# Attention block with two branches: inverse row sums of the last head pair spread by GpSimd and transposed into PSUM, in place of a way through DRAM

## Chip, cores and metric

One NeuronCore of one Trainium2 chip. The metric is device time in microseconds of one execution; the kernel before has three runs.

## What is computed

A block over 512 positions of width 1024. The input is RMS-normalised and projected once; eight heads of forgetting attention (fox) and eight heads of block-sparse attention (moba) follow, each with a SiLU gate, and the two results are projected, gated and added:

```python
proj = rms_norm(x, norm_g) @ w_in
y_fox  = from_heads(fox_attention(q, k, v, log_f)) * jax.nn.silu(fz)
y_moba = from_heads(moba_attention(q, k, v)) * jax.nn.silu(mz)
merged = (sigmoid(ga + b_gate[0]) * (y_fox @ w_fox)
          + sigmoid(gb + b_gate[1]) * (y_moba @ w_moba))
x = x + merged @ w_out
```

With 512 positions and blocks of 256, each moba query sees its own block up to itself and all blocks before it, so both branches are causal softmax attention here. Heads are 64 wide.

## The kernel before

**Precision.** Every matmul operand is split into a high part (rounded by a ScalarE copy, `wh`, `pth`, `yh`) and a low part (a VectorE subtraction, `wl`, `ptl`, `yl`), and a product is three matmuls, high by high, high by low, low by high (two where one operand is stacked).

**Order of the work.** Work is written as a list of units that are interleaved by hand: four attention groups of four heads (fox a, fox b, moba a, moba b), each mixed with projection units as filler, then the gates (`GA`, `GB`), the moba projection (`wm`, matmul tile `pm`) and the output (`wo`, tile `po`). The framework's scheduler then fixes each engine's own queue, which the engine runs strictly in order. The last group's end is interleaved with the first gate product.

**An attention group** handles two pairs of heads, `pr` 0 and 1. For each head, `Aa` makes logits and exponentials `p` with their row sums `rsum`; after each pair, VectorE takes the reciprocals `rinv`, as a column per head and query tile (queries on partitions). `Bb` transposes the exponentials on TensorE in three groups (`p_a` four blocks, `p_b` four, `p_cc` two), splits each (L582, L583), and multiplies them with the values into the bank `pv` (L586, L587). Its two halves are added (`ysh` L611, L612) into `ypair`: 128 partitions are two heads by 64 dimensions, columns are the 512 queries. `Yp` multiplies `ypair` by the SiLU gate `ZS` and the inverse sums, and splits the result into `yh` (L628) and `yl` (L629).

**The inverse sums have to be turned.** `rinv` has queries on partitions; `ypair` has them on columns. So `sums_out` transposes eight columns of `rinv` on TensorE (`p_ri`, L555), copies them out (L557) and stores them to a DRAM tile (L558, 4 KB); `sums_in` loads them back twice with a broadcast over 64 partitions (L566, 128 KB each, ScalarE's queue) into `rinv_bc`. For most pairs GpSimd multiplies gate and sums (L626); for the last pair of the last group VectorE does.

**The gates** use products of half-matrices with sums of them (Strassen-Winograd form: seven products for eight). A product `n` runs 24 matmuls of 128x256 (L715, L717, L718) on one of three PSUM banks, `pb1` to `pb3`. The left sides are the normalised input (`Gh`, `Gl`) and four sums `S0` to `S3`, which GpSimd's queue loads from DRAM (L258) as the attention's tiles become free. ScalarE copies a bank out before it is used again (`e_GA`, L725), VectorE adds it to another (L728). Weights come by SP's queue (L684) into four buffers, are combined by VectorE (L679) and split by L110 on ScalarE and L112 on VectorE, into four further buffers which the products free.

Of the kernel before, what the change touches and what calls it, by code (L numbers as in the profile page):

```python
# [7 lines left out]
F32 = mybir.dt.float32  # L8
F32R = mybir.dt.float32r
AF = mybir.ActivationFunctionType  # L10
OP = mybir.AluOpType
AX = mybir.AxisListType

P = 128
S = 512
D = 1024
NT = S // P
KT = D // P
HD = 64
# [10 lines left out]
def fox_moba_kernel(ctx: ExitStack, tc, xT, x, w_in, w_fl, w_fox, w_moba, w_out, cst, rope, out):  # L30
# [3 lines left out]
    V, A, G, T = nc.vector, nc.scalar, nc.gpsimd, nc.tensor  # L34
# [6 lines left out]
    stage = {}  # L41
# [7 lines left out]
    def t2(tag, bufs, name, shape=(P, 512), dt=F32):  # L49
        pool = stage["pool"] if tag in ("qs", "pt", "pc", "ys") else sb  # L50
        return pool.tile(list(shape), dt, name=name, tag=tag, bufs=bufs)

    def pst(tag, bufs, name):
        return ps.tile([P, 512], F32, name=name, tag=tag, bufs=bufs)
# [4 lines left out]
    def tp(name):  # L59
        return pst("tp", 3, name)  # L60
# [10 lines left out]
    ident = con.tile([P, P], F32, name="ident")  # L71
# [121 lines left out]
    r = con.tile([P, NT], F32, name="r")  # L193
# [191 lines left out]
    ZS = {}  # L385
# [94 lines left out]
    ri = con.tile([P, 16, 4], F32, name="rinv")  # L480
    R_dram = dr.tile([16, NT, P], F32, name="r_dram")

    def attn_group(br, half, gq, gk):
        fox = br == "f"
        qn, kn = QN[f"{br}q{half}"], QN[f"{br}k{half}"]
        hb = 4 * (half == "b") + (0 if fox else 8)
        last = br + half == "mb"
        st = {}
# [32 lines left out]
        def Aa(h):  # L521
            def go():
                qs, kh, kl, q2 = st[h]
                hh = hb + h
                pts = []
                for i in range(NT):
                    n = P * (i + 1)
                    lg = pst("lg", 2, "lg")
                    qt = slice(i * P, (i + 1) * P)
                    T.matmul(lg[:, :n], qs[:, qt], kh[:, :n], start=True, stop=False)  # L530
                    T.matmul(lg[:, :n], q2[:, qt], kl[:, :n], start=False, stop=True)  # L531
                    pt = stage["pool"].tile([P, n], F32, name=f"p{i}", tag=f"p{i}", bufs=2)
                    V.tensor_tensor_reduce(pt, lg[:, :n], mask[:, 512 - n:512], -0.125, 3.0e38,  # L533
                                           op0=OP.add, op1=OP.min, accum_out=mkn[:, hh, i:i + 1])
                    A.activation(pt, pt, AF.Exp, bias=mkn[:, hh, i:i + 1], scale=-1.0,  # L535
                                 accum_out=rs[:, hh, i:i + 1])
                    pts.append(pt)
                st[h] = pts
                if h % 2:
                    inverse_sums(h // 2)  # L540
                elif h:
                    sums_in(0)
            return go
# [8 lines left out]
        def sums_out(pr):  # L552
            h0 = hb + 2 * pr
            p = tp("p_ri")
            T.transpose(p[:8, :P], ri[:, h0:h0 + 2, :].rearrange("p h t -> p (h t)"), ident)  # L555
            rt = sb.tile([8, P], F32, name="rinv_t", tag="rinv_t", bufs=1)
            A.activation(rt, p[:8, :P], AF.Copy)  # L557
            A.dma_start(out=R_dram[h0:h0 + 2].rearrange("h t p -> (h t) p"), in_=rt)  # L558

        def sums_in(pr):  # L560
            if last and pr:
                rb = st["r", pr] = t2("u", 4, "rinv_bc")
            else:
                rb = st["r", pr] = stage["pool"].tile([P, S], F32, name="rinv_bc", tag="rinv_bc", bufs=1)
            for o in range(2):
                A.dma_start(out=rb[o * HD:(o + 1) * HD, :],  # L566
                            in_=R_dram[hb + 2 * pr + o].rearrange("t p -> (t p)").partition_broadcast(HD))

        def Bb(h):
            def go():  # L570
                pts, vt = st[h], VT[f"{br}v{half}"]
                o = h % 2
                pv = pst("pv", 1, "pv")

                def blk(dst, i, j):
                    T.transpose(dst, pts[i][:, j * P:(j + 1) * P], ident)

                def spl(p, n):
                    tag, w, bufs = ("pt", 512, 4) if n == 512 else ("pc", 256, 2)
                    hi = t2(tag, bufs, "pth", (P, w), F32R)  # L580
                    lo = t2(tag, bufs, "ptl", (P, w), F32R)
                    A.activation(hi[:, :n], p[:, :n], AF.Copy)  # L582
                    V.tensor_tensor(out=lo[:, :n], in0=p[:, :n], in1=hi[:, :n].bitcast(F32), op=OP.subtract)  # L583
                    return hi, lo
                def pvm(j, hl, c0, n, start, stop):
                    T.matmul(pv[:, P * j:P * j + n], vt[:, j, h, :], hl[0][:, c0:c0 + n], start=start, stop=False)  # L586
                    T.matmul(pv[:, P * j:P * j + n], vt[:, j, h, :], hl[1][:, c0:c0 + n], start=False, stop=stop)  # L587
                pa = tp("p_a")
                for i in range(4):
                    blk(pa[:, i * P:(i + 1) * P], i, 0)  # L590
                pb = tp("p_b")
                for i in range(1, 4):
                    blk(pb[:, (i - 1) * P:i * P], i, 1)
                blk(pb[:, 384:512], 3, 3)
                ha = spl(pa, 512)
                hbb = spl(pb, 512)
                pc = tp("p_cc")
                for i in range(2, 4):
                    blk(pc[:, (i - 2) * P:(i - 1) * P], i, 2)
                hc = spl(pc, 256)  # L600
                pvm(0, ha, 0, 512, True, False)
                pvm(1, hbb, 0, 384, False, False)
                pvm(3, hbb, 384, 128, False, False)
                pvm(2, hc, 0, 256, False, True)
                pr = h // 2
                if o == 0:
                    st["y", pr] = t2("u", 4, "ypair") if last and pr else t2("ys", 1, "ypair")
                y = st["y", pr]
                me, ot = (slice(0, HD), slice(HD, P)) if o == 0 else (slice(HD, P), slice(0, HD))
                sh = t2("u", 4, "ysh")  # L610
                A.activation(sh[me, :], pv[ot, :], AF.Copy)  # L611
                V.tensor_tensor(out=y[me, :], in0=pv[me, :], in1=sh[me, :], op=OP.add)  # L612
                if o == 0:
                    sums_out(pr)
                elif pr:
                    sums_in(1)
            return go

        def Yp(pr):
            def go():  # L620
                y = st["y", pr]
                gp = 2 * (half == "b") + pr
                yh = t2("y", 15, f"yh{br}{gp}", dt=F32R)
                yl = t2("y", 15, f"yl{br}{gp}", dt=F32R)
                zr = st["r", pr]
                (V if (br, gp) == ("m", 3) else G).tensor_tensor(out=zr, in0=ZS[br, gp], in1=zr, op=OP.mult)  # L626
                V.tensor_tensor(out=y, in0=y, in1=zr, op=OP.mult)
                A.activation(yh, y, AF.Copy)  # L628
                V.tensor_tensor(out=yl, in0=y, in1=yh.bitcast(F32), op=OP.subtract)  # L629
                Y[br, gp] = (yh, yl)  # L630
            return go
# [376 lines left out]
```

## Time and profile before

| | |
|---|---|
| runs | 444.06, 443.63, 441.45 us; median 443.63 |
| profiled execution | 444.28 us, its span 442.5 us |
| mean granted TensorE clock | 0.996 |
| TensorE busy | 428.4 us (97%) |
| VectorE, ScalarE, GpSimd busy | 314.7, 262.5, 87.6 us |
| data moved | 56.40 MB, mean 127 GB/s |

The span runs from the first to the last instruction in the trace; the execution's own time has 1.8 us around it. In the views, PE is TensorE's matmuls, PEld its weight loads, DVE VectorE, ACT ScalarE, POOL GpSimd; SPq and ACTq are instructions that issue transfers. A row of waits reads: engine, tile and line that waited, arrow, what ended the wait, then microseconds in total, times, longest. In the chain and the timeline the first number is the start, the second the duration. A row of groups ends in busy time, mean nanoseconds of one, and idle time ahead.

### The profile page before, as it was taken

Reading aid. Unit: us, or ns where it says so; the run is one execution under the profiler, and the core shown is the slowest. Engines: PE = TensorE matmul, PEld = TensorE weight load, DVE = VectorE, ACT = ScalarE, POOL = GpSimd, SP = SyncE. Lnnn points to the kernel's source line nnn. Section 1 sums busy time; section 2 is a strip of 40 time slices with the busy share of each in tenths; the row PEclk is TensorE's granted clock in tenths of the full one; section 3 lists DMA queues with packets and bytes.
Section 4 is the critical chain, followed back from the end, with each engine's and each line's share of the span. In section 5 each row is a group of like instructions: output and inputs, shape, how many; then the busy total and the mean of one; then the engine's idle time right before and its main releaser. Section 6 shows DMA issues by size and latency. Waiting matters only on the chain.

```text
span 442.5 us, 8082 instructions
## 1 busy us (share of the span) xinstructions
PE 428.4 (97%) x3100; PEld 403.9 (91%) x3100; DVE 314.7 (71%) x563; ACT 262.5 (59%) x491; POOL 87.6 (20%) x106
## 2 busy tenths in 40 slices
PE   6999999999999999999999999987999999999996
PEld 5998899999999998899998878877999989989996
DVE  5559994777998869676956689928978786584311
ACT  5676544876777769887765876717655545531100
POOL 1059200224142950134621002200000000000000
PEclk9999999999999999999999999998999999999999
DMA  8962164424377413303304212663134405624231
GB/s 261 388 246 69 54 205 137 111 74 136 110 233 209 103 55 120 119 13 122 106 14 132 95 24 90 232 203 96 60 133 126 160 1 183 197 96 152 88 96 48
DMA packets 25991, 56.40 MB, mean 127 GB/s; under 512 B 3296, under 2 KB 11936, under 8 KB 25952
## 3 DMA queue, kind: packets, MB, share of 16 engines
q1 hardware_dynamic: 14528, 39.95, 27.4%
q10 hardware_dynamic: 10272, 11.74, 9.0%
q0 software_dynamic: 1152, 4.19, 2.8%
q8 instruction: 24, 0.39, 0.4%
q14 instruction: 15, 0.12, 0.1%
HBM read 46.27 MB, written 6.32 MB: 119 GB/s over the span
## 4 chain that ended last, share of the span: by engine, by line
PE 85%; ACT 6%; DMA 4%; DVE 2%; issue 1%; ACTq 0%; SPq 0%; DVEq 0%
PE pb_GB L718 3%; PE pb_GB L717 3%; PE pb_GB L715 3%; PE po L815 3%; PE po L817 3%; PE po L816 3%; PE pb_GA L715 2%; PE pb_GA L717 2%; PE pb_GA L718 2%; PE pv L587 2%; PE pv L586 2%; PE lg L530 2%; PE lg L531 2%; PE pm L644 2%; PE pm L645 2%; PE pm L646 2%
## 5 line engine op out<-in xcount | busy, mean ns | idle before, releaser
L535 ACT ACTIVATE p<-p,negm 128x128 f32<-128x128 f32 (+1 forms) x64 | 35.7, 558 | 12.5 <-DVE negm L533 11.2
L310 POOL TENSOR_TENSOR ff<-ss,mh 128x8 f32<-128x8 f32 x16 | 27.1, 1699 | 79.6 <-DVE ss L308 77.3
L533 DVE CUSTOM_DVE_ANT_0 p<-lg,mask 128x128 f32<-128x128 f32 (+1 forms) x64 | 30.5, 485 | 5.8 <-PE lg L531 5.6
L815 PE MATMUL po<-wh_wo,mgh 128*128 128x256 f32 x96 | 27.1, 282 | 0.0
L817 PE MATMUL po<-wh_wo,mgl 128*128 128x256 f32 x96 | 27.0, 282 | 0.0
L816 PE MATMUL po<-wl_wo,mgh 128*128 128x256 f32 x96 | 26.9, 281 | 0.0
L825 DVE TENSOR_TENSOR ot<-po,xr 128x256 f32<-128x256 f32 x16 | 6.6, 424 | 24.7 <-PE po L817 23.6
L110 ACT ACTIVATE wh_wo<-wr_wo 128x1024 fp32r<-128x1024 f32 x8 | 8.5, 1061 | 21.6 <-PE po L817 8.0
L530 PE MATMUL lg<-KH,QS 128*128 128x128 f32 (+1 forms) x64 | 20.7, 332 | 0.4 <-DMA KH<-KH 0.4
L112 DVE TENSOR_TENSOR wl_GB<-wr_gb,wh_GB 128x1024 fp32r<-128x1024 f32 x14 | 16.8, 1223 | 4.2 <-ACT wh_GB L110 3.3
L110 ACT ACTIVATE wh_GB<-wr_gb 128x1024 fp32r<-128x1024 f32 x14 | 14.6, 1059 | 8.6 <-PE pm L645 2.5
L612 DVE TENSOR_TENSOR ypair<-pv,ysh 64x512 f32<-64x512 f32 x16 | 11.0, 688 | 10.8 <-ACT ysh L611 10.7
L816 PEld LDWEIGHTS po<-wl_wo,mgh 128*128 128x128 f32 x96 | 18.1, 189 | 0.0
L815 PEld LDWEIGHTS po<-wh_wo,mgh 128*128 128x128 f32 x96 | 18.1, 189 | 0.0
L817 PEld LDWEIGHTS po<-wh_wo,mgl 128*128 128x128 f32 x96 | 18.1, 188 | 0.0
L715 PE MATMUL pb_GA<-Gh,wh_GA 128*128 128x256 f32 x48 | 14.3, 298 | 3.3 <-ACT e_GA L725 3.3
L112 DVE TENSOR_TENSOR wl_GA<-wr_ga,wh_GA 128x1024 fp32r<-128x1024 f32 x14 | 16.6, 1219 | 1.2 <-ACT wh_GA L110 1.1
L110 ACT ACTIVATE wh_GA<-wr_ga 128x1024 fp32r<-128x1024 f32 x14 | 14.5, 1054 | 4.5 <-DVE wr_ga L679 2.7
L504 DVE SCALAR_TENSOR_TENSOR QS<-p_qT,cs,QS 64x512 fp32r<-64x512 f32 x16 | 12.0, 750 | 6.6 <-ACT QS L503 6.2
L611 ACT ACTIVATE ysh<-pv 64x512 f32<-64x512 f32 x16 | 9.5, 593 | 9.8 <-PE pv L587 8.0
L112 DVE TENSOR_TENSOR wl_wo<-wr_wo,wh_wo 128x1024 fp32r<-128x1024 f32 x8 | 9.8, 1222 | 7.4 <-ACT wh_wo L110 7.4
L583 DVE TENSOR_TENSOR ptl<-p_a,pth 128x512 fp32r<-128x512 f32 x16 | 11.0, 687 | 5.1 <-ACT pth L582 5.0
(448 smaller groups left out, 1798.8 us busy)
## 6 DMA issues: line engine op xcount, KB each, us to landing
wr_ga<-in_w_in_dram SPq DMA_DIRECT2D x8, 512.0 KB
wr_gb<-in_w_in_dram SPq DMA_DIRECT2D x8, 512.0 KB
wr_wo<-in_w_out_dram SPq DMA_DIRECT2D x8, 512.0 KB
xt<-in_xT_dram SPq DMA_DIRECT2D x8, 256.0 KB
x<-in_x_dram SPq DMA_DIRECT2D x8, 256.0 KB
s_dramh<-sum_sh ACTq DMA_DIRECT2D x8, 256.0 KB
s_draml<-sum_sl ACTq DMA_DIRECT2D x8, 256.0 KB
KH<-KH ACTq DMA_DIRECT2D x16, 128.0 KB
```

The costliest lines, as they stand in the source:

```text
L110: A.activation(hi[:, :, 0:n], src, AF.Copy)
L112: eng.tensor_tensor(out=lo[:, q, 0:n], in0=src[:, q], in1=hi[:, q, 0:n].bitcast(F32), op=OP.subtract)
L310: G.tensor_tensor(out=f2, in0=ss.rearrange("p t h -> p (t h)"), in1=mh, op=OP.pow)
L530: T.matmul(lg[:, :n], qs[:, qt], kh[:, :n], start=True, stop=False)
L533: V.tensor_tensor_reduce(pt, lg[:, :n], mask[:, 512 - n:512], -0.125, 3.0e38, op0=OP.add, op1=OP.min, accum_out=mkn[:, hh, i:i + 1])
L535: A.activation(pt, pt, AF.Exp, bias=mkn[:, hh, i:i + 1], scale=-1.0, accum_out=rs[:, hh, i:i + 1])
L715: T.matmul(o, hi[:, k, cc], lh, start=(n < 3 and c == 0 and k == 0), stop=False, skip_group_check=True)
L717: T.matmul(o, hi[:, k, cc], ll, start=False, stop=False, skip_group_check=True)
L718: T.matmul(o, lo[:, k, cc], lh, start=False, stop=(k == 3), skip_group_check=True)
L815: T.matmul(p[:, :CW], gh[:, st], hi[:, k, :CW], start=(kk == 0), stop=False)
L816: T.matmul(p[:, :CW], gh[:, st], lo[:, k, :CW], start=False, stop=False)
L817: T.matmul(p[:, :CW], gl[:, st], hi[:, k, :CW], start=False, stop=(kk == KT - 1))
```

## The change

For the last pair of the last group (`last and pr`) alone, the way through DRAM is left out: no `sums_out`, no `sums_in`. In `Yp`, GpSimd copies each head's `rinv` columns, broadcast over 64 columns, into `rinv_w` (two copies of 128x256), TensorE transposes its four 128x128 blocks into a PSUM bank `p_rinv` of the tag `lg`, which the attention's logits no longer need, and VectorE multiplies the gate in place by that bank. All other pairs stay as they were.

```diff
         def sums_in(pr):
             if last and pr:
-                rb = st["r", pr] = t2("u", 4, "rinv_bc")
-            else:
-                rb = st["r", pr] = stage["pool"].tile([P, S], F32, name="rinv_bc", tag="rinv_bc", bufs=1)
+                return
+            rb = st["r", pr] = stage["pool"].tile([P, S], F32, name="rinv_bc", tag="rinv_bc", bufs=1)
...
-                if o == 0:
+                if o == 0 and not (last and pr):
                     sums_out(pr)
...
-                zr = st["r", pr]
-                (V if (br, gp) == ("m", 3) else G).tensor_tensor(out=zr, in0=ZS[br, gp], in1=zr, op=OP.mult)
+                if last and pr:
+                    zr, rb = ZS[br, gp], pst("lg", 2, "p_rinv")
+                    h0 = hb + 2 * pr
+                    rw = t2("u", 4, "rinv_w")
+                    for o in range(2):
+                        G.tensor_copy(rw.rearrange("p (t o d) -> p t o d", o=2, d=HD)[:, :, o, :],
+                                      ri[:, h0 + o, :, None].to_broadcast([P, NT, HD]))
+                    for t in range(NT):
+                        T.transpose(rb[:, t * P:(t + 1) * P], rw[:, t * P:(t + 1) * P], ident)
+                    V.tensor_tensor(out=zr, in0=zr, in1=rb, op=OP.mult)
+                else:
+                    zr = st["r", pr]
+                    G.tensor_tensor(out=zr, in0=ZS[br, gp], in1=zr, op=OP.mult)
                 V.tensor_tensor(out=y, in0=y, in1=zr, op=OP.mult)
```

Lines in the changed kernel are one less after the first edit, and ten more after `Yp`.

## The prediction

> **What bounds the kernel now.** I read the page first, then the waits of the whole span, then the chain of work that ended last and the stretches around the one place it leaves TensorE.
>
> ```profile
> span 442.5 us, 8082 instructions
> PE 428.4 (97%) x3100; PEld 403.9 (91%) x3100; DVE 314.7 (71%) x563; ACT 262.5 (59%) x491; POOL 87.6 (20%) x106
> ```
>
> TensorE is busy for 97% of the span, so only two things can shorten the kernel: less TensorE work, or one of its few gaps closed. The waits, longest first (the first row is TensorE's largest wait of the whole span; none of its waits after it, from 303 us on, is listed at all):
>
> ```profile
> PE pb_GA L715 <- ACT e_GA L725: 3.3, 1, 3.3
> ...
> ACT yhm L628 <- DVE ypair L627: 7.2, 2, 7.0
> ...
> DVE rinv_bc L626 <- DMA rinv_bc<-r_dram: 6.0, 1, 6.0
> ```
>
> Three waits, one cause. The chain shows the order (start, duration, piece):
>
> ```profile
> 284.39 0.28 ACT rinv_t L557
> 284.68 0.27 ACTq L558
> 285.00 1.09 ACT pth L582 x2
> 286.09 0.95 ACT wh_GA L110
> 287.06 1.23 DVE wl_GA L112
> 288.29 0.34 DVE ptl L583
> 288.68 0.40 PE pv L587
> 289.16 0.45 ACTq L566
> 289.65 6.68 DMA rinv_bc<-r_dram
> 296.42 0.70 DVE rinv_bc L626
> 297.15 0.70 DVE ypair L627
> 297.99 0.42 issue
> 298.41 1.99 ACT wh_GA L110 x2
> 300.40 0.49 ACT e_GA L725
> 300.93 0.58 PE pb_GA L715
> ```
>
> The load of the last pair's inverse sums takes 6.68 us. VectorE stands in its queue at L626 for it, ScalarE behind VectorE at the cast L628, and behind that cast stand two weight splits (L110) and the copy L725 that frees the PSUM bank of TensorE's next product. Nobody needs the attention result itself in a hurry: its first reader is a matmul at 345 us.
>
> ```profile
> L644 PE MATMUL pm<-yhm,wh_wm x32: 388/394/403, 345.1 to 394.4; 128*128 128x512 f32 x32
> ```
>
> The stall therefore harms only by what is queued behind it. It has an after-effect in the granted clock (the last columns of a stretch are clock, DMA share, GB/s):
>
> ```profile
> 297.60:300.90 3.30, 0.00 (x0) 0.00 (x0) 2.57 (x4) 3.02 (x5) 0.00 (x0) 0.94 0.00 0
> 300.90:304.00 3.10, 3.07 (x14) 3.07 (x15) 3.07 (x4) 2.70 (x3) 0.00 (x0) 0.51 0.52 153
> 304.00:305.45 1.45, 1.45 (x14) 1.45 (x13) 0.61 (x1) 0.00 (x0) 0.00 (x0) 1.00 0.81 243
> ```
>
> After 3.3 us with no matmul the clock is 0.51 for 3.1 us: 14 matmuls there, where the next 1.45 us holds 14 as well.
>
> **The change, part by part.** In the built program all engines keep their order except around this place. I go by the starts of TensorE's instructions in before:
>
> ```profile
> 282.29 0.40 PE L586 MATMUL pv<-pth,v_mvb 128*128 128x512 f32 x1
> ...
> 283.56 0.28 PE L718 MATMUL pb_GA<-Gh,wl_GA 128*128 128x256 f32 x1
> ...
> 283.92 0.47 PEld L576 LDWEIGHTS p_a<-ident,p 128*128 128x128 f32 x4
> ...
> 285.85 0.48 PE L586 MATMUL pv<-pth,v_mvb 128*128 128x512 f32 x1
> ...
> 288.90 0.28 PE L715 MATMUL pb_GA<-S0h,wh_GA 128*128 128x256 f32 x1
> ...
> 294.58 0.29 PE L715 MATMUL pb_GA<-S1h,wh_GA 128*128 128x256 f32 x1
> ...
> 305.45 0.28 PE L715 MATMUL pb_GA<-S2h,wh_GA 128*128 128x256 f32 x1
> ```
>
> From 288.90 to 294.58 stand 48 gate matmuls (1 + 24 + 23): 0.118 us each, undisturbed.
>
> *Removed ahead of the last head's products.* One transpose, the copy L557 and its store, 0.55 us of ScalarE's chain and about 0.1 of TensorE. The order with it changes: ScalarE now splits the three transposed blocks one after the other (4-block, 2-block, 4-block), and the 1024-wide weight split (0.95 on ScalarE, 1.23 on VectorE), which stood ahead of the third, comes after them. TensorE has 13 gate matmuls between the transposes and the eight pv products in place of 7, since three transposes moved ahead of the previous eight. Those eight took 283.56 - 282.29 = 1.27 unhindered; the last eight took 288.90 - 285.85 = 3.05. Replayed: the copy of the previous products ends near 284.35 as before; the splits on ScalarE take 1.09 for the two wide ones and some 0.4 for the narrow one, to 285.85; VectorE's low half of the last takes
>
> ```profile
> L583 DVE TENSOR_TENSOR ptl<-p_a,pth 128x512 fp32r<-128x512 f32 x16 | 11.0, 687 | 5.1 <-ACT pth L582 5.0
> ```
>
> more, to 286.6 or 286.7; the five products left need some 0.6. The first S0h matmul, 288.90 before, then starts at 287.3: **1.6 us** gained. Bounds: 0 (another wait ends last there) and 3.05 - 1.27 = 1.8.
>
> *Removed: the two loads L566 and the wait for them.* ScalarE's order becomes: copy of bank 1, two weight splits, the copy that frees bank 3, the next split, the copy of bank 1 again, and only then the cast of the attention result. VectorE likewise has its next add and two weight splits ahead of the multiplication by the inverse sums. So bank 3 is freed by: the S0 product done at 287.3 + 48 x 0.118 = 293.0, a split (half of 1.99), the copy (0.5): 294.7. TensorE is there after 72 gate matmuls and the four new transposes, 287.3 + 8.5 + 0.45 = 296.25. The wait at L715 has 1.5 us of cover; without it each late microsecond would cost one. Before, the same 72 matmuls took from 288.90 to 300.93, 12.03 instead of 8.5: **3.5 us** gained.
>
> *The clock.* From 300.93 to 305.45 stand 26 matmuls, 4.52 us; at 0.118 they need 3.08. With no gap ahead of them the loss goes: **1.44 us**. If a shorter gap stays I would expect less loss; bounds 0 and 1.44.
>
> *Added on TensorE: four 128x128 transposes.* Four of the same kind took 0.47 us: **-0.45 us** (the one removed is in the 1.6). The row stands against a rule of the Trainium skill, "TensorE: Matmul & The Clock Gate", Part 4, PE-mode transpose: such a transpose was measured at about 275 ns in a kernel and does not count as busy for the clock. By that rule the four would cost 1.1 us and the sum would be 0.65 smaller; the trace's four, back to back at 0.12 each with full clock around them, speak for the row.
>
> *Added on GpSimd: two copies of 128x256*, last in its queue, after the S3l load that it issues. Durations and landing (the last row's 6.6 us is to landing):
>
> ```profile
> 286.86 0.54 POOL L258 DMA_DIRECT2D S3l<-s_draml  x1
> ...
> L348 POOL TENSOR_TENSOR qn_mqa<-ra,rb 128x128 f32<-128x128 f32 x2 | 0.9, 460 | 0.1
> L312 POOL TENSOR_TENSOR qn_fka<-qn_fka,ff 128x512 f32<-128x512 f32 x2 | 2.5, 1263 | 0.0
> L329 POOL TENSOR_TENSOR tab_mk<-rp,cs 128x64 f32<-128x64 f32 x1 | 1.4, 1384 | 0.0
> ...
> S3l<-s_draml POOLq DMA_DIRECT2D x1, 512.0 KB, 6.6
> ```
>
> No row shows this copy; it lies between 0.46 (half its width, two inputs) and 1.26 (twice its width), and I take 0.65, by the width between those two rows. The load waits for the first pv product, so it goes out near 286.4, and the spread sums are ready near 288.3. The transposes come after 67 gate matmuls, at 295.2: nothing waits. Even if GpSimd were held until S3l has landed (286.4 + 6.6) and each copy took 1.26, it would be 295.5, 0.3 late. TensorE waits in order there, so what is late would stall the S1 product and all behind it.
>
> *Moved on VectorE*: the multiplications by the inverse sums now read PSUM and stand behind two splits; they run near 296 to 297, the casts near 298, and 345 is far. They precede a split needed at about 302 and take 1.4 us; cost nothing under that cover.
>
> *DMA queues*: the two 128 KB loads and one 4 KB store go. Weight loads issued by SP when a split is done come earlier with it. Is what TensorE now reaches 6 us sooner already there? The S tiles and the next weights moved before 295:
>
> ```profile
> 295.00:300.00 5.00, 2.59 (x22) 2.38 (x21) 2.82 (x5) 2.12 (x3) 0.00 (x0) 1.00 0.01 5
> ```
>
> From 295 to 300 the DMA share is 0.01, so they have all landed, and the earliest need is the S2 product, at 299.3 after the change.
>
> **Sum:** 1.6 + 3.5 + 1.44 - 0.45 = 6.1 us. TensorE waits for nothing later in the span, so it keeps all of it: span 442.5 to 436.4, the profiled execution's time 444.28 to 438.2. That execution lies 0.65 above the median of the runs, 443.63; against the median the forecast is **437.5 us**, 1.4% less. About 1% (4.4 us) is what a measurement of this kernel can tell from no change; its runs spread from 441.45 to 444.06.
>
> **The rivals.**
>
> *The pv products still wait* (gain without the 1.6: 4.5, time 439.1). For it: from 285.00 to 288.68 the chain runs without a gap through ScalarE and VectorE, and I replay that to a few tenths only. Against: the two wide splits that stood ahead are behind in the new order.
>
> *The wait at bank 3 stays in part* (439.5 to 441.5, middle 440.5). The new releaser is the end of the S0 product plus a split and a copy, 1.7 us, and TensorE arrives 3.3 us after that end. If ScalarE comes to the splits 3 us late, half the gap and some clock loss remain. Against: what stands ahead of them waits only for TensorE.
>
> *It does not do what it says* (443.6): the wait was covered anyway, and another one at the same place ends last, a late weight chunk for instance. Against: the empty DMA stretch from 295 to 300.
>
> *GpSimd is late, and the kernel slower.* Place: TensorE's first new transpose, at 295.2. At the price of the L329 row, 1.38 us for 64 columns, a copy of 256 takes 5.5 and the two 11.1; behind the landing of S3l (293.0) they end at 304.1, 8.9 us late, plus a clock loss of 1.44 as after the old gap: 443.63 - 6.1 + 10.3 = 447.8. It turns slower than before from 4.7 us late on (6.1 less 1.44), each copy at 3.4 us behind the landing. Against: the L312 row, twice as wide, takes 1.26. On the clock, the Trainium skill ("TensorE: Matmul & The Clock Gate", Part 1) says that an idle window of about 3.4 us drops it to half; the 0.51 after 3.3 us agrees.
>
> **How the numbers follow.** Forecast 0.70; pv products still waiting 0.12; bank 3 in part 0.09; no effect 0.04; GpSimd late 0.05. The forecast's own range, gains of 5 to 7 us and a run's spread of half a microsecond, is 436 to 439.3. For 8 in 10 it has to reach into the first two rivals above and the upper bounds below (1.8 for the first part, no cost of the transposes: 6.7, and a fast run): 435.8 to 440.6. Faster by over 1%, below 439.2: 0.67 of the forecast's 0.70, half of the first rival and a little of the second, together 0.75. Slower by over 1%: little else than late GpSimd, 0.05. Within 1%: 0.20.
>
> **What would show it.** Right: no DMA wait on VectorE near 290; TensorE with no idle over 0.5 us from 289 to 305 and the clock 1.00 there; the eight last pv products within 1.6 us; the first S0h matmul near 287.3 and the first S2h near 299.3; the four transposes in half a microsecond; the two copies over before 290. Wrong: a wait of TensorE for GpSimd at the new transposes, or for L725's copy at the bank; or the gain at the S2 product of 6 us and a smaller one at the end, which would mean that a later stage had another limit.

## The result, and the profile after

| kernel | median us (lowest to highest, runs) | ratio to the kernel before, 95% interval |
|---|---|---|
| before, on that chip | 443.85 (441.45 to 446.05, 6) | |
| changed | 438.18 (435.68 to 440.36, 6) | 0.9861 [0.9828, 0.9894] |

Faster by 1.4%; forecast were 437.5 us and a ratio of 0.986. The profiled execution of the changed kernel is one of the slower of its runs: 440.36 us, span 438.7. Its head, and TensorE's longest waits of the whole span:

```profile
span 438.7 us, 8086 instructions
PE 427.1 (97%) x3103; PEld 402.8 (92%) x3103; DVE 314.6 (72%) x563; ACT 262.5 (60%) x490; POOL 90.4 (21%) x108
...
PE fqa L358 <- ACT Zh L101: 2.8, 1, 2.8
PE warm_ps L82 <- DVE fg_pre L446: 1.6, 1, 1.6
PE pv L585 <- ACT pth L581: 1.2, 2, 0.7
```

The 3.3 us at the gate product, TensorE's largest wait before, is not there any more; what leads the list now stands ahead of the change (the rows are waits at 8, at 1.6, and at 188 and 263 us). (L725, L727 and L728 are the gate's matmuls here, L735 the copy of the bank, L632 the new transposes.) TensorE around the change, instruction by instruction:

```profile
289.34 0.28 PE L725 MATMUL pb_GA<-S0h,wh_GA 128*128 128x256 f32 x1
...
297.30 0.60 PE L632 MATMUL p_rinv<-ident,rinv_w 128*128 128x128 f32 x4
...
298.33 0.28 PE L725 MATMUL pb_GA<-Gh,wh_GA 128*128 128x256 f32 x1
...
301.40 0.28 PE L725 MATMUL pb_GA<-S2h,wh_GA 128*128 128x256 f32 x1
```

298.33 is the start of the sixth product, the one that waited for bank 3. The same stretch in a view by windows, cut at the first gate matmul `pb_GA` (281.73), the first of the last eight `pv` products, the first S0h, the sixth product and the first S2h (columns: stretch, length, busy time and count of PE, PEld, DVE, ACT, POOL, then clock, DMA share, GB/s):

```profile
281.73:287.17 5.44, 5.36 (x44) 5.11 (x42) 5.41 (x10) 4.47 (x9) 1.07 (x2) 1.00 0.46 169
287.17:289.34 2.17, 1.88 (x8) 1.19 (x9) 2.17 (x4) 0.90 (x1) 1.19 (x2) 1.00 0.84 264
289.34:298.33 8.99, 8.99 (x79) 8.99 (x77) 4.58 (x6) 3.80 (x5) 0.94 (x2) 1.00 0.76 280
298.33:301.40 3.07, 3.07 (x29) 3.07 (x28) 2.83 (x5) 2.92 (x4) 0.00 (x0) 1.00 0.50 171
```

From 289.34 to 301.40 TensorE has no gap at all and the clock is 1.00. Nearly all the idle time is in the second stretch: 1.88 busy of 2.17 us, and VectorE busy for all of it. From the first gate matmul to the first S2h this trace gained 5.16 us where the sum has 6.1. Of the 0.94 it is short, 0.72 lies in that stretch (0.88 gained for 1.6) and 0.21 in the one ahead of it.

### The profile page after: what moved, and what is told of

Same layout as the page of the kernel before. It is cut to its first block, busy times and chain, and to the rows that moved or that the text cites. A ratio compares the mean times of both kernels' runs of the same rounds, so it can differ in the third digit from the quotient of the medians.

```text
span 438.7 us, 8086 instructions
## 1 busy us (share of the span) xinstructions
PE 427.1 (97%) x3103; PEld 402.8 (92%) x3103; DVE 314.6 (72%) x563; ACT 262.5 (60%) x490; POOL 90.4 (21%) x108
## 5 line engine op out<-in xcount | busy, mean ns | idle before, releaser
L530 PEld LDWEIGHTS lg<-KH,QS 128*128 128x128 f32 x64 | 12.1, 189 | 2.0 <-ACT pth L581 1.4
```

## The experiments

All are compared by the same marks, starts of TensorE's matmuls in each trace, so that what happened earlier in an execution drops out. A is the first gate matmul `pb_GA` (the expectations call it the first A11 matmul), then the last eight pv products, S0h, the sixth product, S2h; the last column reaches to S3h, the eighth product's first matmul. Rows in us:

| trace | A to pv | pv to S0h | S0h to sixth | sixth to S2h | A to S2h | A to S3h |
|---|---|---|---|---|---|---|
| before | 5.23 | 3.05 | 12.03 | 4.52 | 24.83 | 30.28 |
| before, again | 5.39 | 2.91 | 12.55 | 5.63 | 26.48 | 31.93 |
| changed | 5.44 | 2.17 | 8.99 | 3.07 | 19.67 | 25.10 |
| changed, again | 5.20 | 1.56 | 8.98 | 3.06 | 18.80 | 24.24 |
| changed, third | 5.20 | 1.58 | 8.97 | 3.07 | 18.82 | 24.26 |
| DRAM way, read late | 5.23 | 3.05 | 8.53 | 3.08 | 19.89 | 25.33 |
| DRAM way, turned and read late | 5.20 | 1.57 | 8.54 | 3.08 | 18.39 | 23.83 |
| the same, again | 5.20 | 1.56 | 8.53 | 3.10 | 18.39 | 23.83 |
| GpSimd multiplies | 5.23 | 3.04 | 11.32 | 3.19 | 22.78 | 28.22 |

The run with a filled gap is not in the table, since its sixth product is split; it is measured from S1h.

The first four runs below shared one chip (before there: 445.65 us median, 442.86 to 446.73), the last four another (before: 443.60, 440.71 to 445.81).

### The changed kernel again

No edit. The question is whether 5.16 us from A to S2h, where the sum has 6.1, is the mechanism or one execution.

> The changed kernel once more, for a second trace. Theory (the replay was right, the profile was taken in an execution with a late start of the last head): the eight last pv products take about 1.5 us and the gain from the first A11 matmul to the first S2h matmul is 5.2 to 6.1 us against 24.83 in before. Rival (the first term of the sum was mis-sized): the burst takes again about 2.2 us and the gain is again about 5.2.

Measured: 438.44 us (437.66 to 439.05), ratio 0.9843 [0.9814, 0.9872].

```profile
280.20:285.40 5.20, 5.20 (x44) 5.12 (x42) 5.17 (x10) 3.62 (x6) 1.07 (x2) 1.00 0.61 220
285.40:286.96 1.56, 1.53 (x10) 1.11 (x9) 1.16 (x3) 1.06 (x1) 0.87 (x2) 1.00 0.79 205
286.96:295.94 8.98, 8.98 (x79) 8.98 (x77) 5.39 (x6) 3.80 (x5) 1.41 (x2) 1.00 0.78 285
295.94:299.00 3.06, 3.06 (x28) 3.06 (x27) 2.82 (x5) 2.91 (x4) 0.00 (x0) 1.00 0.51 171
```

The second stretch is 1.56 instead of 2.17, the third and fourth are as in the first trace. A to S2h is 6.03 us less than before. So the sum of 6.1 holds in full against the trace it was made from, and the burst of pv products is the part that differs between these two executions of the changed kernel.

### The DRAM way kept, its reader late

The prediction's reading was that the load from DRAM harms only by what is queued behind its reader. Then the load may stay, if the reader stands behind the work that TensorE needs. VectorE's order is the scheduler's, so the edit gives the multiplication a true dependency: a 1.0 worked out from the copy of bank 3.

```diff
-    Y = {}
+    Y, LATE = {}, {}
...
-                (V if (br, gp) == ("m", 3) else G).tensor_tensor(out=zr, in0=ZS[br, gp], in1=zr, op=OP.mult)
+                if last and pr:
+                    one = sb.tile([P, 2, 4], F32, name="one", tag="ss", bufs=4)[:, 0, 0:1]
+                    V.tensor_scalar(one, LATE["e"][:, 0:1], 0.0, 1.0, op0=OP.mult, op1=OP.add)
+                    V.scalar_tensor_tensor(zr, ZS[br, gp], one, zr, op0=OP.mult, op1=OP.mult)
+                else:
+                    G.tensor_tensor(out=zr, in0=ZS[br, gp], in1=zr, op=OP.mult)
...
+            if name == "GA0" and n == 3:
+                LATE["e"] = st["e", n]
```

> The kernel before with its way through DRAM and its order of the pv products; only the multiplication by the inverse sums reads a 1.0 derived from the copy of bank 3 (L725), so that it and what follows it stand behind the weight splits and that copy in VectorE's and ScalarE's queues. Theory (the wait harms only by what is queued behind it): the gap of 3.3 us ahead of the sixth product and the slow clock go, 3.5 + 1.44 = 4.9 us, so about 438.9 against 443.85. Rival (the sums have to come sooner, the way through DRAM itself is what costs): no gain, 443.5 to 444.

Measured: 438.39 us (438.16 to 440.04), ratio 0.9848 [0.9823, 0.9873]. Windows, cut at the pv burst, S0h, the sixth product and S2h, then the copy of the bank and the late multiplication:

```profile
284.72:287.77 3.05, 2.08 (x12) 1.27 (x10) 2.63 (x4) 1.45 (x3) 1.07 (x2) 1.00 0.87 266
287.77:296.30 8.53, 8.53 (x73) 8.53 (x73) 4.26 (x6) 3.80 (x5) 0.00 (x0) 1.00 0.83 272
296.30:299.38 3.08, 3.08 (x28) 3.08 (x27) 2.99 (x5) 2.99 (x4) 0.00 (x0) 1.00 0.52 170
...
294.49 0.58 ACT L730 ACTIVATE e_GA<-pb_GA 128x512 f32<-128x512 f32 x1
...
L629 DVE SCALAR_TENSOR_TENSOR rinv_bc<-zs_mzb,one,rinv_bc x1: 753/753/753, 295.9 to 295.9; 128x512 f32<-128x512 f32 x1
```

The pv burst is 3.05, exactly as before: that term is untouched, as it should be, for the transpose and the store are still ahead of it. The gap is gone, 8.53 for 72 matmuls, and the clock stays 1.00. The trace gains 4.94 us from A to S2h, and the way through DRAM was not made faster. The time fell by more than the expected 4.9, by 7.3 us (the interval reaches from 5.7 to 7.9); the second trace of before, below, bears on that. The run separates the terms: the wait and the clock come from the order, not from the way.

### The DRAM way, turned behind the last products and read very late

Both halves at once, without GpSimd and without the four transposes. The one transpose, its copy and its store are written behind the last head's products (in the trace the transpose stands among them, at 285.11), and the reader waits for a later copy, so that it runs at 312.5 us and not at 295.9 (there is room: the result is first read at 345 us in before).

```diff
-                if o == 0:
+                if o == (1 if last and pr else 0):
                     sums_out(pr)
-                elif pr:
+                if o and pr:
                     sums_in(1)
...
-            if name == "GA0" and n == 3:
+            if name == "GA1" and n == 3:
                 LATE["e"] = st["e", n]
...
-        if n == 2:
+        if n == 10:
             gate[0]()
```

(The last two hunks are against the experiment above.)

> The kernel before with its way through DRAM, but the sums are turned only after the last pv products, and the multiplication stands behind the bank copy of the second gate group; the order of the pv products is that of the changed kernel, with no transposes of the spread sums. Theory: all of the changed kernel's gain, and the 0.45 us of its four transposes less 0.1 for the one of the sums: 0.3 to 0.4 below the changed kernel, about 437.8 against 443.85. Rival (the sums must come by GpSimd and TensorE for the gain): not below 442.

Measured: 437.02 us (436.4 to 438.27), ratio 0.9817 [0.979, 0.9843].

```profile
284.47:286.04 1.57, 1.57 (x11) 1.21 (x10) 1.17 (x3) 1.21 (x2) 0.54 (x1) 1.00 0.83 224
286.04:294.58 8.54, 8.54 (x74) 8.54 (x73) 3.81 (x5) 3.68 (x5) 0.00 (x0) 1.00 0.75 265
294.58:297.66 3.08, 3.08 (x29) 3.08 (x27) 2.64 (x3) 2.83 (x3) 0.00 (x0) 1.00 0.72 221
```

All three terms are here with the DRAM way still in use: 1.57, 8.54, 3.08. Against the changed kernel the third stretch is 0.44 shorter, the four transposes. A to S3h is 23.83 where the changed kernel takes 24.24.

### Twelve more matmuls in the gap

The clock term by itself: the kernel before, with the gap partly filled by matmuls that compute nothing needed.

```diff
+            if name == "GA0" and n == 5:
+                fb = pst("lg", 2, "fill")
+                for i in range(12):
+                    T.matmul(fb[:, :HT], B[3][0][:, 3, P:2 * P], left("S2", 3)[0], start=(i == 0), stop=(i == 11))
```

> The kernel before with 12 more matmuls of 128x256 into an unused bank, in the gap ahead of the sixth gate product (their result is not used; the second half of that product moves behind the next one with it). Theory (the slow clock follows from the gap of 3.3 us and costs 1.44): the gap shrinks to about 2 us, the granted clock stays near 1.00 behind it, and the time falls by up to 1.4 us to about 442.4, although work was added. Rival (the slow matmuls have another cause, the clock would come back by itself): clock again near 0.5 behind the gap, 443.5 to 444.

Measured: 442.11 us (440.94 to 443.61), ratio 0.9928 [0.99, 0.9956]. The fill, the gap that is left, and the sixth product's first part:

```profile
297.79:299.37 1.58, 1.58 (x14) 1.37 (x12) 0.88 (x2) 1.28 (x2) 0.00 (x0) 1.00 0.00 0
299.37:301.15 1.78, 0.00 (x1) 0.01 (x1) 1.75 (x3) 1.78 (x4) 0.00 (x0) 1.00 0.00 0
301.15:304.00 2.85, 2.85 (x24) 2.85 (x25) 2.69 (x4) 1.38 (x2) 0.00 (x0) 1.00 0.52 160
```

TensorE still waits for the bank (1.78 us), nothing was taken away, and work was added; yet the kernel is faster. The matmuls behind the gap run at clock 1.00: 24 in 2.85 us, where before had 14 in 3.10. The scheduler put half of the sixth product behind the S2 product, so the whole is measured from S1h to S3h: 14.73 us instead of 16.32, 1.59 less. Of that, 0.13 is the sixth product's earlier start (11.90 us behind S0h for 12.03), and 1.46 is left for the clock. So the clock term exists apart from the gap. The time moved more than the expected 1.4 us, 445.65 to 442.11 (the interval reaches from 2.0 to 4.5): the next experiment bears on that.

### The kernel before again

No edit: is 1.44 us the clock loss of this kernel, or of one execution?

> The kernel before once more, for a second trace on a chip where the others run. Theory (the terms are those of the first trace): the load of the sums takes 6 to 8 us, TensorE's gap ahead of the sixth gate product is 3 to 4.5 us with a clock near 0.5 behind it, and from the first A11 matmul to the first S3h matmul it is 30.3 us as in the first trace or up to 1.5 more. Rival (the gap of the first trace was an exception): a gap under 1.5 us.

Measured: 444.58 us (441.41 to 445.74), ratio 1.0013 [0.9984, 1.0043]. TensorE's wait, the load in the chain, and windows of the gap and of the sixth product:

```profile
PE pb_GA L715 <- ACT e_GA L725: 3.9, 1, 3.9
...
289.47 7.19 DMA rinv_bc<-r_dram
...
297.25:301.27 4.02, 0.16 (x3) 0.00 (x1) 3.26 (x5) 3.06 (x5) 0.00 (x0) 0.84 0.00 0
301.27:304.00 2.73, 2.73 (x13) 2.73 (x13) 2.70 (x4) 2.66 (x3) 0.00 (x0) 0.50 0.49 153
304.00:306.90 2.90, 2.90 (x15) 2.90 (x15) 0.98 (x2) 0.00 (x0) 0.00 (x0) 0.52 0.59 216
```

The load took 7.19 us, not 6.68; the gap was 3.9, not 3.3; and the slow clock lasted through the whole sixth product, 5.63 us for what takes 3.08: 2.55 lost instead of 1.44. The same program, the same place, 1.65 us more from A to S2h. So the loss of the kernel before is not one number. It also bears on the times above. From A to S3h the kernels of the other runs gain more against this second trace than against the first:

| kernel | against the first trace | against the second | time |
|---|---|---|---|
| changed, three traces | 5.2 to 6.0 | 6.8 to 7.7 | 5.7, 7.2, 6.0 |
| DRAM way, read late | 4.95 | 6.60 | 7.3 |
| DRAM way, turned and read late, two traces | 6.45 | 8.10 | 8.6, 6.1 |
| twelve more matmuls (S1h to S3h) | 1.59 | 3.23 | 3.5 |

The times that lay above the expectations lie nearer to the second trace. That fits a loss that is often larger than 1.44; two traces of before do not show how often. The run of the next experiment does not follow it: 2.06 and 3.71 in the traces, 0.9 in the time.

The mean granted clock of whole executions points the same way, with less weight than it seems to have. For before it was 0.9922 on average over the 11 runs on one chip and 0.9930 over the 23 on the other; the changed kernel has 0.9982 over 4, 0.9973 over 6, and 0.9963 over the 6 of the first comparison. But the mean also takes in the start of an execution. In the third trace of the changed kernel the clock is 0.50 from 9 to 11 us, and the mean 0.995, though around the change the clock is 1.00. In the first trace of before the matmuls from 9 to 11 us start 0.21 us apart, as slowly, where 0.12 is full speed, and the clock column says 1.00 there. So a mean can be lower by some thousandths in an execution that is not slower.

### GpSimd multiplies the last pair's sums

The other way to keep VectorE out of the wait: the multiplication goes to GpSimd as for all other pairs.

```diff
-                (V if (br, gp) == ("m", 3) else G).tensor_tensor(out=zr, in0=ZS[br, gp], in1=zr, op=OP.mult)
+                G.tensor_tensor(out=zr, in0=ZS[br, gp], in1=zr, op=OP.mult)
```

> The kernel before, only that GpSimd in place of VectorE multiplies the gate by the loaded sums. VectorE then adds the second bank ahead of the wait, and ScalarE has one weight split ahead of its cast of the attention result, while the second split and the bank copy stay behind that cast. Theory (what counts is ScalarE's queue, where the bank copy stands behind the cast): the gap stays, cast at about 299, bank free at 300.9 as before; time within 0.5 us of before. Rival (VectorE standing at the load is what counts): the gap shrinks by 2 us or more and the time falls by 2 to 5 us.

Measured: 442.75 us (440.84 to 445.81), ratio 0.9988 [0.9962, 1.0014]: no difference to be seen. The chain and the windows of the gap and the sixth product:

```profile
288.74 6.26 DMA rinv_bc<-r_dram
295.11 1.32 POOLq L1004
296.46 0.70 DVE ypair L627
...
297.72 1.04 ACT wh_GA L110
298.76 0.49 ACT e_GA L725
299.30 0.39 PE pb_GA L715
...
296.55:299.30 2.75, 0.14 (x3) 0.01 (x1) 2.75 (x4) 2.12 (x4) 0.00 (x0) 1.00 0.02 6
299.30:302.49 3.19, 3.19 (x27) 3.19 (x27) 2.96 (x3) 2.66 (x3) 0.00 (x0) 1.00 0.80 257
```

The chain has the same links as before. VectorE no longer waits for the load, but its next instruction, the one on `ypair`, waits for GpSimd, and ScalarE's cast, the split and the bank's copy stand behind that. GpSimd takes 1.32 where VectorE took 0.70, one split (0.95) less stands behind the cast, and this load was 0.42 shorter: the gap shrinks by 0.7 us. (POOLq L1004 in the chain stands where GpSimd's multiplication runs.) In this trace A to S3h is 2.06 less, most of it because the clock stayed at 1.00. But it is one of the quicker of the kernel's runs, 441.30 against a median of 442.75; the runs allow a gain of 1.7 us at most. The outcome lies near the theory of the expectation: moving the waiting instruction to another engine did not help here, because its successor in the same in-order queue waits for it.

### Both again, to compare them

> The changed kernel beside the next one on one chip, for the comparison. Both theories: about 438.3.

> The kernel with the way through DRAM, turned after the last pv products and used late, beside the changed kernel. Theory: 0.4 us below it in the trace from the first A11 to the first S3h matmul (23.8 against 24.2), and 0.4 to 1.5 below it in time. Rival (the lower time of the first run was chance): equal within 0.3.

Measured: the changed kernel 437.63 us (436.93 to 439.01), ratio 0.9875 [0.9842, 0.9908]; the DRAM way turned and read late 437.51 us (436.21 to 438.99), ratio 0.9869 [0.9834, 0.9903]. In the traces the latter is ahead by 0.43 us from A to S3h, as in the first pair (0.41). In time it was ahead by 1.4 us in one comparison and by 0.1 in the other, where 0.4 to 1.5 was expected: by time alone the second comparison came out as the rival had it. The intervals overlap in both, so 0.4 us is a reading of four traces, which the times do not contradict and do not resolve.

## Why the prediction was right, point by point

**The wait at bank 3: 3.5 us less, predicted and found.** With the transposes in it, S0h to the sixth product was predicted to shrink by 3.5 - 0.45 = 3.05 and shrank by 3.04, 3.05 and 3.06. The cover was sized well too: the bank's copy was to be over 1.5 us before TensorE comes, and is over at 296.66, 1.67 us before 298.33:

```profile
296.08 0.58 ACT L735 ACTIVATE e_GA<-pb_GA 128x512 f32<-128x512 f32 x1
...
297.94 0.69 DVE L633 TENSOR_TENSOR zs_mzb<-zs_mzb,p_rinv 128x512 f32<-128x512 f32 x1 [0.51 <-PE p_rinv L632]
...
299.90 0.62 ACT L638 ACTIVATE yhm<-ypair 128x512 fp32r<-128x512 f32 x1
```

The multiplication and the cast now come behind that copy, which is the reordering that the sum rests on. The rival of a wait that stays in part found nothing: 72 gate matmuls and four transposes in 8.99 us, all of it busy (the view's 79 counts those that reach over its edges).

**The clock: 1.44 predicted, 1.45 and 1.46 found against the trace that I summed from.** The mechanism holds by itself (the fill). The size is that of one execution of before: another lost 2.55, and its gap was 0.6 longer. The forecast was a sum over one execution, so that it came within 0.7 us of the first comparison is partly luck: against the second trace of before the same change gains 7.7 us in two of three traces, and the three comparisons of times have 5.7, 7.2 and 6.0.

**The burst of pv products: 1.6 predicted, 0.67 in the first trace, 1.5 in the other two.** (Counted from A to S0h, since the first trace loses 0.21 ahead of the burst.) This step was mis-sized for one execution out of three. The chain of the first trace in that stretch:

```profile
284.70 1.13 DVE wl_GA L112
285.83 0.60 DVE ylm L639
286.43 0.59 DVE ypair L611
287.02 0.13 DVE ptl L582
...
287.54 1.01 DVE ptl L582 x2
```

VectorE works through a queue without a pause, and the low halves `ptl` come last in it. Counted from A, its `ypair` there starts at 4.62 us in the timeline where before had it at 3.77: VectorE, not TensorE, was late in that execution. The trace shows where it lost the time, with the same place in the second trace below it (L689 combines weights, L636 multiplies gate and sums of the pair before):

```profile
271.45 1.29 POOL L636 TENSOR_TENSOR rinv_bc<-zs_mzb,rinv_bc 128x512 f32<-128x512 f32 x1 [27.32 <-DMA rinv_bc<-r_dram]
271.57 2.25 DVE L689 TENSOR_TENSOR wr_ga<-wr_ga,wr_ga 128x1024 f32<-128x1024 f32 x1
...
270.07 1.22 DVE L689 TENSOR_TENSOR wr_ga<-wr_ga,wr_ga 128x1024 f32<-128x1024 f32 x1
270.57 1.89 POOL L636 TENSOR_TENSOR rinv_bc<-zs_mzb,rinv_bc 128x512 f32<-128x512 f32 x1 [28.18 <-DMA rinv_bc<-r_dram]
```

In the first trace GpSimd began 0.12 us ahead and VectorE's instruction took 1.03 longer. In the second and third VectorE began 0.5 us ahead and kept its 1.22, and GpSimd took 0.6 longer. Behind L689 VectorE has hardly a pause up to the burst, so it could not make the time up. GpSimd starts there when a load lands, so the order of the two differs between executions, and the change has no part in it. The second trace of before has the same late L689 (2.20 us) and lost next to nothing by it: 8.30 from A to S0h against 8.28. No run holds this order fixed, so that the late L689 is the reason rests on these traces. My replay followed ScalarE's splits and one low half of VectorE; it left out that VectorE's other work stands ahead of that half. This is the rival of pv products that still wait, in one execution and in part: 0.9 of its 1.6 us, 0.2 of that ahead of the burst. The same execution also came to A 1.1 us later than before's, by waits far ahead of the change, and gave back 0.25 behind S2h: 5.16 - 1.11 - 0.25 = 3.8, its difference in span. Taken from that trace alone the change would have looked two thirds its size.

**The four transposes: 0.45 predicted, 0.44 found.** Tile views of the changed kernel's first trace and of its second:

```profile
L632 PE MATMUL p_rinv<-ident,rinv_w x4: 272/272/273, 297.3 to 297.6; 128*128 128x128 f32 x4
...
L629 POOL COPY rinv_w<-rinv x2: 390/824/1257, 288.7 to 289.9; 128x256 f32<-128x256 f32 x2
...
L629 POOL COPY rinv_w<-rinv x2: 406/903/1400, 286.6 to 287.0; 128x256 f32<-128x256 f32 x2
```

The 0.47 us of the prediction came from a row of weight loads (PEld); the transposes of that row themselves start at 284.02 in before, the next group at 284.46, which is the 0.44 that was found. One transpose lasts 0.272 us from start to end, and that is about the 275 ns that the Trainium skill ("TensorE: Matmul & The Clock Gate", Part 4, PE-mode transpose) gives for bf16; these are fp32. The number fits and my use of it as a rival price was wrong: the four overlap, start 0.11 us apart and hold TensorE for 0.44. That transposes do not count as busy no run here can show, since gate matmuls stand close on both sides.

**GpSimd: 0.65 per copy predicted, 0.4 alone and 1.26 to 1.40 beside a weight split found.** The bounds were 0.46 and 1.26, so both lie at their edges or just outside; the value between them was no real duration. It did not matter: the copies end at 290.29 and are needed at 297.30, 7 us of cover, 6.5 in the second trace. The rival of a late GpSimd had the right place and a price far off.

**It does what it says.** The empty DMA stretch was read rightly: nothing that TensorE reaches six us sooner was late. From 302 to 330 us it is busy without a pause in all of these traces.

**The signs that were named.** The second and third traces meet them: the eight products within 1.6 us, S0h at 286.96 and 287.29, S2h at 299.00 and 299.33, the copies over by 289, no gap from there to 305. The first trace meets those of the gap, the clock and the transposes and misses the others: 2.17 us, 289.34, 301.40, and copies that end at 290.29.

## What to carry to other kernels

A wait is charged to the instruction that stands in it, but its price is what is queued behind it in the same in-order queue; ask who is behind, and whether the waiting one is urgent at all. Here moving the reader of a slow transfer behind urgent work, and its start out of a busy chain, gave as much as replacing the transfer (in the traces 0.4 us more), while handing the wait to an idle engine gave nothing that the times show. Before a sum is made against one profiled execution, take a second trace of the same kernel: here the same stretch was 1.65 us longer in it, and the mean granted clock of whole executions (0.996 where the average was 0.993) could only hint at that.

## What the runs showed of the hardware

**How long a gap costs clock.** Gaps at the same place, and what came behind: 1.8 us (the fill) and 2.6 us (GpSimd multiplies), clock 1.00; 3.3 us (before), 0.51 for 3.1 us, 1.44 us lost; 3.9 us (before, again), 0.50 to 0.52 for the 5.6 us up to S2h, where the matmuls are 0.12 us apart again, 2.55 lost. So shortening a gap from 3.3 to 2.6 us removed the after-effect whole in that trace, though the gap was still most of what it had been.

Length alone does not decide it. Near 7 us, ahead of `fqa`, TensorE waits in every trace, and in four of them the clock from 9 to 11 us is 0.50 to 0.57 behind a wait of 2.2 us (DRAM way turned and read late, the second run), 2.6 (GpSimd multiplies), 2.7 and 2.8 us (changed, second and third). So in the one trace of "GpSimd multiplies" two waits of 2.6 us stand, one with the after-effect and one without. Ahead of the one at `fqa` TensorE had worked for under 4 us, so the two places are not alike. The Trainium skill ("TensorE: Matmul & The Clock Gate", Part 1) explains the step by an activity window of about 3.4 us that runs freely and halves the clock after an idle one, so that the onset depends on where the window happens to lie. The varying onset agrees with that; that a whole window has to be idle does not, since the gaps of 3.3 and of 2.2 to 2.8 us are shorter than one. These traces do not show where the limit is.

**A GpSimd copy and a VectorE subtraction take turns.** In the second trace of the changed kernel:

```profile
286.57 1.55 DVE L112 TENSOR_TENSOR wl_GA<-wr_ga,wh_GA 128x1024 fp32r<-128x1024 f32 x1 [0.40 <-ACT wh_GA L110]
286.62 1.75 POOL L629 COPY rinv_w<-rinv 128x256 f32<-128x256 f32 x2
```

The split took 1.55 us instead of its usual 1.22, a little less than the length of the first copy (0.41) more, and the second copy, begun at 287.0, lasted 1.40 and ended 0.3 us after the split did. The third trace has the same durations. In the first trace a copy that began 0.2 us behind the split took 1.26 and ended just after it, the split kept its 1.21, and the copy behind took 0.39. The Trainium skill ("SBUF — State Buffer", Who interferes with whom and, for the blocking, SBUF: two separate sides) says that a VectorE instruction with two inputs in SBUF contends with a GpSimd instruction that reads SBUF, and that the engine which comes second is blocked for the whole instruction. The first trace fits that, and so does the pair L636 and L689 above, where the one that began second took longer in each trace. In the second trace the three take turns too, but the first copy's record begins 0.05 us behind the split's and it was the split that was held up, so who came first is not to be read there. A small GpSimd copy has therefore two prices in these traces, and which one it gets depends on what VectorE does beside it.
